# Weight pieces split once and kept in DRAM, and the rotary step of attention moved from GpSimd to VectorE

## The chip, the cores and the metric

The program runs on one core of a Trainium2 chip. The metric is the device time of one execution in microseconds. The kernel before took 1531.3 us (median of three runs, 1529.03 to 1531.97). TensorE is called PE here, its weight loads PEld, VectorE DVE, ScalarE ACT, GpSimd POOL and SyncE SP, as in the profile. PE, DVE, ACT and POOL each work through one queue in order; SP issues most of the DMAs, POOL issues some, among them all that add to their destination.

## The reference

One layer of a streaming encoder, on 2048 prompt tokens and 32 sample tokens, 1024 features, all in float32:

```
h  = RMSNorm(x);  z = h @ W_in          # q k v gA B C u gB mA mB, 5376 columns
q, k = rope(rmsnorm(q)), rope(rmsnorm(k))          # per head of 64; 8 q heads, 2 kv heads
yA = (attend(q, k, v) * silu(gA)) @ W_A # own chunk of 64 tokens and the two before, with sinks
yB = (B * conv3(C * u) * silu(gB)) @ W_B
r  = x + (sigmoid(mA) * yA + sigmoid(mB) * yB) @ W_o
out = r + sigmoid(r @ W_pg) * (p @ W_pp)

rope(x): x1, x2 = halves of the head;  [x1*cos - x2*sin, x2*cos + x1*sin]
rmsnorm(x): x * rsqrt(mean(x*x) + eps) * g
```

The rotary step and the root of the norm belong to one another: the root is one number for each token and head, so it can be multiplied in before the rotation or after it.

## The kernel before, in words

Every float32 product is computed as three matmuls on values split in two: a value v becomes h, v rounded to the format of the matmul, and l = v - h. ACT makes h by a cast and DVE makes l by a subtraction. Weights come from DRAM in pieces of 128 x 512 floats (256 KB, `wr`), four blocks of 128 x 128 each; a piece is split into a tile `w` with both halves. The input `wu` holds the weights in units of eight blocks, so a unit is two pieces. Many products use Strassen-like sums, which take seven products (numbered 1 to 7) for eight; products 1, 2 and 4 use a piece of the weights as it is, products 3, 5, 6 and 7 use sums of pieces, which the kernel forms once and keeps in DRAM (`ws` and `qs`).

The kernel has two parts.

**The steps** (up to about 855 us) compute z = h @ W_in in 21 groups of columns, first for tokens 0 to 1023 (pass 0, products in steps named (0, g, p)) and then for the others (pass 1, steps (1, g, p), with sets of smaller products before and between them). Their results pass through tiles of the pool `tp` (14 tiles named "t", from `tmp`) on their way to DRAM. The order of instructions here is made by the framework's own scheduler from the order in which the program names the work.

**The units** (after that) do attention and the products yB, yA, o (W_o), pg (W_pg) and pp (W_pp), in four blocks of tokens: 0, the two big blocks 1 and 2 together (unit kind "B"), and 3, which ends with quarter-size products (kind "S"). PE goes through the units in the order of the list `plan`. The rest is put into each engine's queue by a planner in the kernel: it keeps a clock of PE (`now`), estimated costs of every operation, and counts of buffers; a task runs when its time is due and its buffers are free, and `next_loads` issues loads ahead of PE. The queues that come out are fixed when the program is built.

**Weights in the units.** `next_loads` loads each piece into one of 8 raw tiles (tag "wf") and `split_w` splits it on ACT and DVE into one of 5 tiles "w". Some pieces are loaded and split several times: those of W_A in blocks 0, 1 with 2, and 3, for instance.

**Attention.** The function `attention` handles 128 tokens (16 such tiles, and one of the 32 sample tokens). PE transposes q, k and v into PSUM (`pq`, `pkv`). ACT squares them into `qn`; DVE sums the squares (`ss`) and adds eps; POOL takes the power -0.5 of `ss` and multiplies the table of cosines and sines `cs` by the gains (`ab`). DVE multiplies q and k by the root into `qn`. POOL multiplies `qn` by `ab` into `tt` (each value times its cosine and times its sine) and adds the halves into `kr` and `qr`. PE transposes `kr` and `qr`, and scores, softmax and the product with V follow.

The attention code that the change replaces on POOL:

```
for h0, hn, q in ((8, 2, 1), (0, 8, 0)):
    eG.tensor_tensor(out=tt[:n, h0:h0 + hn], in0=qn[...], in1=ab[:n, q]..., op=mul)
```

## Time and profile before

| | |
|---|---|
| median of three runs | 1531.3 us |
| the profiled execution | 1532.24 us, its span 1530.5 us |
| PE busy | 1501.7 us (98% of the span) |
| PE weight loads | 1333.8 us (87%) |
| DVE busy | 1206.2 us (79%) |
| ACT busy | 836.3 us (55%) |
| POOL busy | 468.3 us (31%) |
| moved by DMA | 357.94 MB, 234 GB/s over the span |
| granted PE clock | 0.995 |

How to read it: matmuls overlap one another, so a mean duration of one matmul is longer than the time between two of them, and PE's busy time is the union. What PE could still lose or win is its idle time and the time in which the clock is not granted. "Idle before" of a group names what that engine waited for. The table of stretches gives busy time of every engine, the granted clock, the share of time in which the 16 DMA engines were busy (packets of several queues can overlap, so it can exceed 1) and the rate.

### The profile page before, as it was taken

How to read it: one execution, taken by the hardware profiler on the slowest of the kernel's cores; microseconds unless marked ns; L12 is line 12 of the kernel's file. 1: busy time of each engine (PE TensorE's matmuls, PEld its weight loads, DVE VectorE, ACT ScalarE, POOL GpSimd, SP SyncE). 2: the span in 40 equal slices, each digit the busy share in tenths (PEclk: the TensorE clock that was granted, in tenths of full speed). 3: DMA queues.
4: the chain of work that ended last, by engine and by line, in shares of the span. 5: the costliest groups of instructions: out<-in, count | busy, mean ns of one | idle time of the engine just before them, and what ended most of it. 6: DMA issues, size and time to landing. Idle time of an engine off the chain costs nothing.

```text
span 1530.5 us, 27077 instructions
## 1 busy us (share of the span) xinstructions
PE 1501.7 (98%) x9025; PEld 1333.8 (87%) x9025; DVE 1206.2 (79%) x2208; ACT 836.3 (55%) x1966; POOL 468.3 (31%) x634
## 2 busy tenths in 40 slices
PE   9999999999999999999999999989999999999898
PEld 7878888888889999999999889978887877888898
DVE  7896887875589766898955787898967789785886
ACT  8453354344467544434554566767775475653575
POOL 2133332332212232333232245462433334112112
PEclk9999999999999999999999999999999999999999
DMA  9479886798778845343555786685678838879998
GB/s 341 154 280 342 308 293 232 276 342 279 241 266 268 307 141 196 117 132 115 184 191 185 266 302 216 217 245 188 201 193 217 220 93 205 223 209 319 289 311 253
DMA packets 207292, 357.94 MB, mean 234 GB/s; under 512 B 24624, under 2 KB 61552, under 8 KB 207152
## 3 DMA queue, kind: packets, MB, share of 16 engines
q1 hardware_dynamic: 165216, 252.40, 50.9%
q0 software_dynamic: 32288, 85.99, 19.3%
q10 hardware_dynamic: 9648, 17.83, 3.1%
q8 instruction: 71, 1.16, 0.3%
q14 instruction: 69, 0.57, 0.1%
HBM read 238.77 MB, written 117.46 MB: 233 GB/s over the span
## 4 chain that ended last, share of the span: by engine, by line
PE 41%; DVE 5%; DMA 4%; issue 2%; ACT 1%; SPq 0%; POOL 0%; DVEq 0%; ACTq 0%
PE b L135 7%; PE yB L135 6%; PE yA L135 3%; PE o L135 3%; PE pg L135 3%; PE O L135 2%; DMA pf<-in_pT 2%; PE S L135 2%; PE s58a L135 1%; PE la L722 1%; DMA wr<-in_wu 1%; PE a L589 1%; PE a L586 1%; PE a L584 1%; PE s50a L135 1%
## 5 line engine op out<-in xcount | busy, mean ns | idle before, releaser
L586 PE MATMUL a<-x_l,w 128*128 128x264 f32 (+1 forms) x744 | 228.2, 319 | 0.0
L584 PE MATMUL a<-x_h,w 128*128 128x264 f32 (+1 forms) x744 | 227.3, 320 | 0.4 <-DVE s L790 0.4
L589 PE MATMUL a<-x_h,w 128*128 128x264 f32 (+1 forms) x744 | 201.4, 320 | 0.0
L135 ACT CAST w<-wr 128x512 fp32r<-128x512 f32 x204 | 123.7, 621 | 87.2 <-PE b L135 30.9
L135 DVE TENSOR_TENSOR w<-wr,w 128x512 fp32r<-128x512 f32 x204 | 154.0, 765 | 18.3 <-ACT w L135 16.8
L206 ACT CAST w<-wr 128x512 fp32r<-128x512 f32 (+1 forms) x180 | 110.1, 618 | 105.8 <-PE c L589 30.7
L207 DVE TENSOR_TENSOR w<-wr,w 128x512 fp32r<-128x512 f32 (+1 forms) x180 | 131.0, 738 | 36.9 <-ACT w L206 35.6
L584 PEld LDWEIGHTS a<-x_h,w 128*128 128x128 f32 x744 | 139.8, 188 | 11.0 <-DVE s L790 0.6
L586 PEld LDWEIGHTS a<-x_l,w 128*128 128x128 f32 x744 | 140.1, 188 | 10.3
L135 PE MATMUL b<-xb_h,w 128*128 128x512 f32 x448 | 142.7, 395 | 1.8 <-ACT w L135 1.1
L589 PEld LDWEIGHTS a<-x_h,w 128*128 128x128 f32 x744 | 125.2, 188 | 10.8
L722 PE MATMUL la<-x_h,w 128*128 128x264 f32 x516 | 111.9, 285 | 1.7 <-ACT w L206 1.2
L584 PE MATMUL c<-x_h,w 128*128 128x512 f32 (+1 forms) x336 | 110.5, 339 | 0.0
L586 PE MATMUL c<-x_l,w 128*128 128x512 f32 (+1 forms) x336 | 110.4, 338 | 0.0
L135 PEld LDWEIGHTS b<-xb_h,w 128*128 128x128 f32 x448 | 83.4, 188 | 21.0 <-DVE w L135 1.6
L206 ACT CAST w<-a 128x512 fp32r<-128x512 f32 x82 | 49.7, 620 | 94.3 <-DVE a L342 30.9
L589 PE MATMUL c<-x_h,w 128*128 128x512 f32 (+1 forms) x336 | 99.9, 338 | 0.0
L783 DVE SCALAR_TENSOR_TENSOR u<-u,c 128x264 f32<-128x264 f32 (+1 forms) x125 | 59.4, 507 | 42.7 <-ACT u L778 28.4
L778 ACT COPY u<-a 128x264 f32<-128x264 f32 (+1 forms) x114 | 47.4, 437 | 79.7 <-PE a L589 75.5
L135 PE MATMUL yA<-ac_h,w 128*128 128x512 f32 (+1 forms) x320 | 89.0, 358 | 1.6 <-DVE ta L135 1.0
L722 PEld LDWEIGHTS la<-x_h,w 128*128 128x128 f32 x516 | 87.0, 189 | 2.4 <-ACT w L206 1.4
L135 PE MATMUL b<-xb_l,w 128*128 128x512 f32 x224 | 88.3, 394 | 0.0
(535 smaller groups left out, 4310.2 us busy)
## 6 DMA issues: line engine op xcount, KB each, us to landing
wr<-in_wu SPq DMA_DIRECT2D x213, 256.0 KB, 4.2
a<-in_wu SPq DMA_DIRECT2D x116, 256.0 KB, 5.1
wr<-ws SPq DMA_DIRECT2D x74, 256.0 KB, 3.5
wr<-qs SPq DMA_DIRECT2D x64, 256.0 KB, 4.6
ws<-a POOLq DMA_DIRECT2D x63, 256.0 KB, 3.8
qs<-a POOLq DMA_DIRECT2D x24, 256.0 KB, 5.7
tb<-z_t SPq DMA_DIRECT2D x24, 256.0 KB, 4.9
z_t<-tb SPq DMA_DIRECT2D x24, 256.0 KB, 4.3
```

The costliest lines, as they stand in the source:

```text
L135: return f(**kw)
L206: nc.scalar.copy(out=hi, in_=src)
L207: nc.vector.tensor_tensor(out=lo, in0=src, in1=hi.bitcast(F32), op=sub)
L584: nc.tensor.matmul(out=ps[:, :cn], lhsT=w[:, 0, k], rhs=x[0][:, c0:c0 + cn], start=first and k == 0, stop=False, skip_group_check=True)
L586: nc.tensor.matmul(out=ps[:, :cn], lhsT=w[:, 0, k], rhs=x[1][:, c0:c0 + cn], start=False, stop=False, skip_group_check=True)
L589: nc.tensor.matmul(out=ps[:, :cn], lhsT=w[:, 1, k], rhs=x[0][:, c0:c0 + cn], start=False, stop=k == 3, skip_group_check=True)
L722: nc.tensor.matmul(out=ps[:, :m], lhsT=w[:, a, k], rhs=r[:, cols], start=q in "ABG" and j == 0 and e == 0, stop=j == 1 and e == 2, skip_gr ...
L778: nc.scalar.copy(out=t[:, c0:c0 + cn], in_=ps[:, :cn])
L783: nc.vector.scalar_tensor_tensor(out=t[:, c0:c0 + cn], in0=t[:, c0:c0 + cn], scalar=-1.0, in1=ps[:, :cn], op0=mul, op1=sub)
```

## The change

**Stored pieces.** 52 pieces (W_B and W_A of all eight units, W_pp, W_o and W_pg) get a place in DRAM for both halves (`stored`, tiles `wd`, 512 KB each). `store_split` takes three tiles of `tp`, loads a piece on SP, splits it on ACT and DVE, and stores both halves by two DMAs from POOL. The table `store_at` puts these 52 into the steps: 28 into pass 0 from group 9 on, 4 into (1, 5..8, 6), and 20 into groups 16 to 20 of pass 1.

**Units.** Where a piece is stored (`unit_key`), the units load both halves: 512 KB into a "w" tile by one DMA, or into two "wf" tiles by two DMAs, without ACT and DVE. In the built program 128 loads of 256 KB with their splits become 128 loads of 512 KB; the 64 loads of sums `qs` are still split. `room` counts the tiles.

**Plan.** yB and pp of block 2 and 3 alternate; pp of block 3 (n = 2 to 5) moves from the end of the big blocks to between the yA of block 0; yA of block 3 begins earlier among the last products of the big blocks. Two loads of rows of p fall away.

**Attention.** ACT's squares go to a tile `sq` that stands for the whole run and has eps in a 65th column, so that DVE's sum includes it. DVE multiplies q and k out of PSUM by `ab` into `tt`, adds the halves into `kn` and `qr`, and multiplies these by the root at the end (`kr`, `qr`). POOL keeps the power, and `ab`, which is now formed before the squares.

```diff
+    def store_split():
+        u, e = to_store.pop(0)
+        raw = tmp(f"wq{u}_{e}")[:, :512]
+        nc.sync.dma_start(out=raw, in_=wu[u, :, 4 * e:4 * e + 4, :].rearrange("p a b -> p (a b)"))
+        h, lo = [tmp(f"wq{x}{u}_{e}", F32R)[:, :512] for x in "hl"]
+        split(h, lo, raw)
+        for i, v in enumerate((h, lo)):
+            nc.gpsimd.dma_start(out=stored[u, e][:, i], in_=v.bitcast(F32).rearrange("p (a b) -> p a b", a=4))
...
+    store_at = {(0, g, p): 1 for g in range(9, G) for p in (6, 3) if p == 6 or g > 11}
+    store_at.update({(0, g, 5): 1 for g in range(14, G)})
+    store_at.update({(1, g, p): 1 for g in range(5, 9) for p in (6,)})
+    store_at.update({(1, g, p): 1 for g in range(16, G) for p in (1, 6, 7, 5)})
...
-        while n_raw[0] < len(worder) and busy["Y"] < now[0] + 0.5 and (
-                n_raw[0] < RAWS or raw_free[n_raw[0] - RAWS] <= now[0]) and n_raw[0] < len(made) + RAWS:
-            i = n_raw[0]
+        while n_load[0] < min(len(worder), used[0] + LOOK) and busy["Y"] < now[0] + 0.5:
+            i = n_load[0]
+            key = worder[i]
...
+            if unit_key(key):
+                where = "w" if room["w"] > len(to_split) else "wf"
+                if where == "wf" and room["wf"] < 3:
+                    break
+                src = stored[unit_key(key)]
+                tiles = w_tiles(i, where)
+                if where == "w":
+                    eY.dma_start(out=whole[i].bitcast(F32), in_=src)
+                else:
+                    for v in range(2):
+                        eY.dma_start(out=tiles[v].bitcast(F32), in_=src[:, v])
+                w_ready[i] = fin[0] + 0.5
...
-    plan += tail[:21]
-    for e, part in enumerate(tail[21:]):
-        plan += [part, ("yA", 3, NA[3][e])]
-    plan += [("pp", 3, 2), ("pp", 3, 3), ("yA", 3, NA[3][7]), ("pp", 3, 4), ("pp", 3, 5)]
+    plan += tail[:17]
+    late = [("yA", 3, n) for n in NA[3]]
+    for e, part in enumerate(tail[17:27]):
+        plan += [part] + ([late.pop(0)] if e not in (2, 9) else [])
+    plan.append(tail[27])
...
         for h0, hn, src in q3:
-            eS.activation(out=qn[:n, h0:h0 + hn], in_=src[:n], func=AF.Square, scale=SCALE)
+            eS.activation(out=sq[:n, h0:h0 + hn, 0:64], in_=src[:n], func=AF.Square, scale=SCALE)
...
+        for q, (h0, hn, src) in enumerate(q3):
+            eV.tensor_tensor(out=tt[:n, h0:h0 + hn], in0=src[:n].unsqueeze(2).to_broadcast([n, hn, 2, 64]),
+                            in1=ab[:n, q].unsqueeze(1).to_broadcast([n, hn, 2, 64]), op=mul)
...
-        eV.tensor_reduce(out=ss[:n], in_=qn[:n], axis=AX.X, op=add)
-        eV.tensor_scalar(out=ss[:n], in0=ss[:n], scalar1=EPS, scalar2=None, op0=add)
+        eV.tensor_reduce(out=ss[:n], in_=sq[:n], axis=AX.X, op=add)
...
+        for d in (0, 32):
+            for o, h in ((kn, slice(8, 10)), (qr, slice(0, 8))):
+                eV.tensor_tensor(out=o[:n, :, d:d + 32], in0=tt[:n, h, 0, d:d + 32], in1=tt[:n, h, 1, 32 - d:64 - d], op=add)
...
-        for h0, hn, src in q3[::-1]:
-            eV.tensor_tensor(out=qn[:n, h0:h0 + hn], in0=src[:n], op=mul,
-                            in1=ss[:n, h0:h0 + hn].unsqueeze(2).to_broadcast([n, hn, 64]))
...
-        for h0, hn, q in ((8, 2, 1), (0, 8, 0)):
-            eG.tensor_tensor(out=tt[:n, h0:h0 + hn],
-                            in0=qn[:n, h0:h0 + hn].unsqueeze(2).to_broadcast([n, hn, 2, 64]),
-                            in1=ab[:n, q].unsqueeze(1).to_broadcast([n, hn, 2, 64]), op=mul)
...
+        eV.tensor_tensor(out=kr[:n], in0=kn[:n].unsqueeze(2).to_broadcast([n, 2, 2, 64]),
+                        in1=ss[:n, 8:10].unsqueeze(2).unsqueeze(3).to_broadcast([n, 2, 2, 64]), op=mul)
+        eV.tensor_tensor(out=qr[:n], in0=qr[:n], in1=ss[:n, 0:8].unsqueeze(2).to_broadcast([n, 8, 64]), op=mul)
```

**How the queues move.** Three places. The first is the rotary step of the first tile of block 2 (names with `2_0`), on POOL, before:

```order
L135 TENSOR_TENSOR ss2_0_12274<-ss2_0_12274,nhalf_70 128x10
L135 TENSOR_TENSOR ab2_0_12316<-cs2_0_12091,cst_69 128x256
L135 DMA ta0_4_12121<-z_t1_4_112 128x512
L135 TENSOR_TENSOR tt2_0_12383<-qn2_0_12261,ab2_0_12316 128x256
L135 DMA ta0_5_12166<-z_t1_5_113 128x512
L135 TENSOR_TENSOR tt2_0_12383<-qn2_0_12261,ab2_0_12316 128x1024
L135 TENSOR_TENSOR kr2_0_12385<-tt2_0_12383 128x4x32 x2
L135 TENSOR_TENSOR qr2_0_12384<-tt2_0_12383 128x8x32 x2
L135 COPY KH_10068<-KH_10068 128x2x128
L135 COPY KL_10069<-KL_10069 128x2x128
```

and on POOL now:

```order
L135 TENSOR_TENSOR ab2_0_12757<-cs2_0_12656,cst_69 128x256
L135 DMA ta0_3_12574<-z_t1_3_111 128x512
L135 TENSOR_TENSOR ss2_0_12796<-ss2_0_12796,nhalf_70 128x10
L135 DMA ta0_4_12649<-z_t1_4_112 128x512
L135 COPY KH_10522<-KH_10522 128x2x128
L135 COPY KL_10523<-KL_10523 128x2x128
```

The products and sums of the rotation are gone from POOL; the power `ss` and `ab` have stayed. On DVE the same tile now has these rows (`m0` are values of block 0 being split, `pf` rows of p, `ta` the yA of block 0, `VL` the low half of v, `at` and `ptl` attention of earlier chunks):

```order
L135 TENSOR_TENSOR tt2_0_12763<-pq2_0_12749,ab2_0_12757 128x1024
L135 TENSOR_TENSOR tt2_0_12763<-pkv2_0_12754,ab2_0_12757 128x256
L135 TENSOR_REDUCE ss2_0_12796<-sq_10534 128x10
L135 SCALAR_TENSOR_TENSOR m0_1_l_12773<-ta0_1_12430,m0_1_h_12772 128x512
...
L135 TENSOR_TENSOR kn2_0_12765<-tt2_0_12763 128x2x32
L135 TENSOR_TENSOR qr2_0_12764<-tt2_0_12763 128x8x32
L135 TENSOR_TENSOR kn2_0_12765<-tt2_0_12763 128x2x32
L135 TENSOR_TENSOR qr2_0_12764<-tt2_0_12763 128x8x32
L135 TENSOR_TENSOR ptl_13_0_12874<-PT_13_0_12868,pth_13_0_12873 128x512
L135 TENSOR_TENSOR kr2_0_12766<-kn2_0_12765,ss2_0_12796 128x256
L135 TENSOR_TENSOR qr2_0_12764<-qr2_0_12764,ss2_0_12796 128x512
```

where it had two products before, `qn` out of PSUM by the root, between which and POOL's rows nothing else of the tile stood on DVE:

```order
L135 SCALAR_TENSOR_TENSOR m0_2_l_12326<-ta0_2_12014,m0_2_h_12325 128x512
L135 TENSOR_TENSOR qn2_0_12261<-pkv2_0_12253,ss2_0_12274 128x128
L135 TENSOR_TENSOR qn2_0_12261<-pq2_0_12248,ss2_0_12274 128x512
L135 SCALAR_TENSOR_TENSOR ta0_5_12166<-ta0_5_12166,yA0_5_0_12285 128x512
L135 TENSOR_TENSOR KL_10069<-pk1_3_12328,KH_10068 128x2x128
```

So DVE has nine rows of the rotation instead of two, the first two of which read PSUM and wait for no root.

The second place is SP late in pass 0, at the loads of group 19 (`a19`), before:

```order
L330 DMA wr130_3775<-in_wu 128x512
L330 DMA a19_0_3832<-in_wu 128x512
L330 DMA a19_1_3834<-in_wu 128x512
L330 DMA a19_2_3836<-in_wu 128x512
L330 DMA a19_3_3838<-in_wu 128x512
L330 DMA wr136_3904<-in_wu 128x512
```

and now, with `wq` the pieces to be stored (their stores, two each, stand on POOL):

```order
L334 DMA wr130_3963<-in_wu 128x512
L334 DMA a19_0_4044<-in_wu 128x512
L334 DMA a19_1_4046<-in_wu 128x512
L374 DMA wq49_0_3825<-in_wu 128x512
L334 DMA a19_2_4048<-in_wu 128x512
L334 DMA a19_3_4050<-in_wu 128x512
L374 DMA wq66_0_3851<-in_wu 128x512
```

Loads of pieces to be stored stand between the loads that the group itself needs. The third place is SP at the change from W_o to W_pg in block 3 (units "S"; `z_r` and `r` are rows of r), before:

```order
L135 DMA wr520_17514<-in_wu 128x512
L135 DMA wr521_17535<-in_wu 128x512
L135 DMA z_r1_93<-r013_0_17069 128x544
L135 DMA wr522_17559<-in_wu 128x512
L135 DMA wr523_17567<-in_wu 128x512
L135 DMA z_r5_97<-r113_1_17207 128x544
L135 DMA wr524_17591<-in_wu 128x512
```

and now:

```order
L135 DMA w520_17765<-wd67_1_164 128x1024
L135 DMA w521_17787<-wd58_0_173 128x1024
L135 DMA wh522_17790<-wd58_1_189 128x512
L135 DMA wl522_17791<-wd58_1_189 128x512
L135 DMA w523_17811<-wd59_0_174 128x1024
L135 DMA w524_17831<-wd59_1_190 128x1024
```

Each of these pieces is now 128 x 1024 floats, in one load or in two.

More of the change, by code (lines that the diff above doesn't have):

```diff
@@ L1191, in tile_hybrid_stream_step @@
             quad_sums(*sums_at[todo[0]])
+        for _ in range(store_at.get(todo[0], 0)):
+            store_split()
         if i in after:
@@ L1218, in tile_hybrid_stream_step @@
         nc.gpsimd.memset(v.bitcast(F32), 0.0)
+    sq = att.tile([P, 10, 65], F32, tag="sq", name="sq")
+    nc.gpsimd.memset(sq, EPS)
     restart()
@@ L1779, in run_big @@
         for k in range(4):
-            while ("XB", x, p, k) not in have or wi >= len(w_ready) or w_ready[wi] > now[0]:
+            while ("XB", x, p, k) not in have or w_ready.get(wi, 1e9) > now[0]:
                 idle()
-            hi, lo = made[wi][:, 0, k], made[wi][:, 1, k]
+            hi, lo = [v[:, k] for v in W2[wi]]
             xh, xl = XB[x, p, k]
@@ L1793, in run_big @@
                 free("kx", 2)
-        over.add(widx.pop(wk))
-        while n_done[0] in over:
-            n_done[0] += 1
+        w_over(wk)
         go(big_done(u, ps), now[0] + SEM, BIG_NEED.get((x, p)), -1)
@@ L2076, in run_quads @@
                 i, half = XP[p]
-                while ("X", x, i, k) not in have or wi >= len(w_ready) or w_ready[wi] > now[0]:
+                while ("X", x, i, k) not in have or w_ready.get(wi, 1e9) > now[0]:
                     idle()
@@ L2089, in run_quads @@
                 if k == 3:
-                    over.add(widx.pop(wk))
-                    while n_done[0] in over:
-                        n_done[0] += 1
+                    w_over(wk)
         for n, p in u["parts"]:
@@ L2160, in tile_hybrid_stream_step @@
     widx = {}
-    n_raw, n_hi, n_made, n_done = [raws[0]], [len(made)], [len(made)], [used[0]]
-    landed = {i: 3.0 for i in range(raws[0])}
-    raw_free = [6.0 if i < len(made) else 1e9 for i in range(raws[0])]
-    w_ready = [0.5] * len(made)
-    base = used[0]
+    W2 = {i: (made[i][:, 0], made[i][:, 1]) for i in range(used[0], len(made))}
+    w_ready = {i: 0.5 for i in W2}
+    room = {"w": WB - len(W2), "wf": 8}
+    slot = {i: "w" for i in W2}
+    n_load, to_split, landed, whole = [len(made)], [], {}, {}
     def w_of(key, u):
@@ L2231, in tile_hybrid_stream_step @@
+            n_load[0] += 1
+        if to_split and landed[to_split[0]] <= now[0] and room["w"] > 0 and now[0] >= hold[0] and busy["S"] < now[0] + (
+                0.3 if to_split[0] > used[0] + 2 else 1.5):
+            go(split_w(to_split.pop(0)))
     work = [0.0]
     last_use = {k: x for x, u in enumerate(units) for k in u["w"]}
-    over = set()
     def run_units():
@@ L2257, in run_units @@
                     wi = w_of(wk, u)
-                    while key not in have or wi >= len(w_ready) or w_ready[wi] > now[0]:
+                    while key not in have or w_ready.get(wi, 1e9) > now[0]:
                         idle()
                     k = i % 4 + (2 * (u["n"] % 2) if wk[0] == "pp" else 0)
-                    hi, lo = made[wi][:, 0, k], made[wi][:, 1, k]
+                    hi, lo = [v[:, k] for v in W2[wi]]
                     a = operand(key)
```

127 lines of the change are left out of this document (74 added, 53 removed).

## The prediction, made before the changed kernel was run

> **What bounds the kernel now.** I read the busy times first, then the stretches of the span in which PE is idle, then what PE waits for, and last what DVE and POOL do at those moments. The page's first line:
>
> ```profile
> PE 1501.7 (98%) x9025; PEld 1333.8 (87%) x9025; DVE 1206.2 (79%) x2208; ACT 836.3 (55%) x1966; POOL 468.3 (31%) x634
> ```
>
> PE is the bound, and the change leaves its matmuls alone. All that can be won is idle PE time, 1530.5 - 1501.7 = 28.8 us, plus lower-clock time. The stretches show where it lies (length, busy time of PE, PEld, DVE, ACT and POOL, then the granted clock, the share of busy DMA engines and the rate):
>
> ```profile
> 325.00:350.00 25.00, 25.00 (x110) 20.28 (x109) 17.86 (x30) 10.92 (x20) 7.04 (x13) 1.00 0.98 354
> 337.00:465.00 128.00, 128.00 (x634) 107.57 (x632) 86.48 (x160) 64.02 (x120) 25.92 (x49) 1.00 0.79 266
> 465.00:525.00 60.00, 57.76 (x463) 56.50 (x462) 50.75 (x104) 42.41 (x96) 18.39 (x28) 1.00 0.88 304
> 750.00:850.00 100.00, 99.42 (x816) 99.21 (x815) 63.93 (x133) 54.79 (x117) 21.46 (x24) 1.00 0.63 205
> 1000.00:1034.00 34.00, 28.21 (x158) 23.96 (x157) 33.43 (x48) 20.79 (x59) 21.40 (x22) 1.00 0.84 223
> 1155.00:1175.00 20.00, 17.13 (x82) 13.37 (x82) 16.92 (x26) 14.24 (x44) 11.22 (x11) 0.91 0.90 264
> 1240.00:1265.00 25.00, 21.77 (x107) 17.51 (x106) 22.38 (x35) 17.00 (x47) 13.99 (x16) 1.00 0.37 96
> 1400.00:1436.00 36.00, 30.59 (x204) 27.62 (x203) 29.69 (x59) 17.72 (x36) 7.84 (x9) 1.00 1.08 317
> 1433.00:1525.00 92.00, 89.19 (x688) 87.90 (x688) 76.63 (x152) 59.53 (x126) 15.67 (x18) 0.98 0.95 288
> ```
>
> In the steps (to 855 us) PE hardly idles. Three stretches of attention lose 5.8, 2.9 and 3.2 us, 11.9 in all; 1400 to 1436 us loses 5.4. PE's two longest waits (total, times, longest), then DVE and then POOL around them (start, duration):
>
> ```profile
> PE S L135 <- DVE qs L135: 5.5, 2, 3.8
> PE yA L135 <- DVE ac_l L135: 2.9, 1, 2.9
> ```
> ```profile
> 1006.37 3.79 DVE L135 TENSOR_TENSOR w<-wr,w 128x512 fp32r<-128x512 f32 x2
> ...
> 1023.50 0.68 DVE L135 SCALAR_TENSOR_TENSOR m_l<-ta,m_h 128x512 fp32r<-128x512 f32 x1
> 1027.24 4.92 DVE L135 SCALAR_TENSOR_TENSOR m_l<-ta,m_h 128x512 fp32r<-128x512 f32 x1
> 1165.33 4.74 DVE L135 SCALAR_TENSOR_TENSOR ac_l<-acf,ac_h 128x512 fp32r<-128x512 f32 x2
> ```
> ```profile
> 1026.09 0.89 POOL L135 DMA_DIRECT2D ta<-z_t  x1 [0.82 <-DVE KL L135]
> 1026.69 2.70 POOL L135 TENSOR_TENSOR tt<-qn,ab 128x1024 f32<-128x1024 f32 x1
> 1029.06 1.15 POOL L135 TENSOR_TENSOR kr<-tt 128x128 f32<-128x128 f32 x2
> 1029.89 1.65 POOL L135 TENSOR_TENSOR qr<-tt 128x256 f32<-128x256 f32 x2
> 1165.55 3.35 POOL L135 TENSOR_TENSOR tt<-qn,ab 128x256 f32<-128x256 f32 x2
> ```
>
> The same DVE instruction takes 0.68 us alone and 4.92 us while POOL runs `tt`, `kr`, `qr`; it ends (1032.16) as they do (1031.54). DVE is 98% busy in that stretch, so `qs`, queued behind it, comes late, and PE with it. The second wait has the same form. So the unit losses from 1000 to 1265 us come from POOL's rotary step holding up DVE.
>
> From 1400 us it is something else. The chain of waits there runs through DMAs (start, length):
>
> ```profile
> 1373.44 10.34 DMA wr<-in_wu
> ...
> 1392.56 7.58 DMA ta<-z_t
> 1400.15 11.15 DMA pf<-in_pT
> ...
> 1413.38 7.94 DMA pf<-in_pT
> ```
>
> against a usual landing of 4.2 us (the page: `wr<-in_wu SPq DMA_DIRECT2D x213, 256.0 KB, 4.2`), in a stretch whose DMA share is 1.08.
>
> **The change part by part.** Three groups of rows carry the counts (instructions, busy time, mean ns; from 855 us on):
>
> ```profile
> L135 ACT CAST w<-wr 128x512 fp32r<-128x512 f32 x188 | 114.0, 621 | 79.5 <-PE b L135 30.9 <-PE yA L135 16.2 <-PE yB L135 11.3
> L135 DVE TENSOR_TENSOR w<-wr,w 128x512 fp32r<-128x512 f32 x188 | 143.4, 771 | 16.8 <-ACT w L135 15.4 <-DMA wr<-in_wu 0.5
> L135 DVE TENSOR_TENSOR qn<-pq,ss 128x512 f32<-128x512 f32 x16 | 10.9, 680 | 0.0
> L135 DVE TENSOR_TENSOR KL<-pk,KH 128x256 fp32r<-128x256 f32 x16 | 6.7, 416 | 1.0 <-ACT KH L135 1.0
> L135 DVE TENSOR_TENSOR qn<-pkv,ss 128x128 f32<-128x128 f32 x16 | 4.5, 284 | 0.1
> L135 DVE TENSOR_TENSOR VL<-pkv,VH 64x64 fp32r<-64x64 f32 x64 | 14.1, 220 | 2.8 <-ACT vo L135 1.3 <-ACT VH L135 0.7
> L135 POOL TENSOR_TENSOR tt<-qn,ab 128x1024 f32<-128x1024 f32 x16 | 41.8, 2613 | 0.0
> L135 POOL TENSOR_TENSOR ss<-ss,nhalf 128x10 f32<-128x10 f32 x16 | 32.7, 2044 | 114.8 <-DVE ss L135 100.0 <-DVE se L135 14.7
> L135 POOL TENSOR_TENSOR qr<-tt 128x256 f32<-128x256 f32 x32 | 27.1, 929 | 0.0
> L135 POOL TENSOR_TENSOR kr<-tt 128x128 f32<-128x128 f32 x32 | 21.4, 771 | 0.0
> ```
>
> *A: the rotary step, with the splits of the units.* POOL loses 2.6 us of `tt`, 1.9 of `qr` and 1.5 of `kr` a tile, beside the small `tt`. DVE gains two products out of PSUM, four sums and two multiplications. The product of 1024 does not stand in the trace: from the rows of 512 and 256 elements the slope is (0.680 - 0.416)/256, so 0.680 + 512 slopes = 1.21 us (twice 0.680 at most). The rest: `tt` of 256, 0.42; sums, 2 x 0.22 and 2 x 0.42; `kr`, 0.42; `qr`, 0.68. Together 4.0 us, less the two `qn` rows and the addition of eps (some 1.1): +2.9 a tile, about 49 us over 17 tiles. Against it stand 128 splits: 128 x 0.771 = 98.7 us of DVE and 128 x 0.621 = 79.5 of ACT. DVE is lighter by about 50 us in the units, and its long blocks lose their partner. What that can bring is the idle time of the three stretches, 11.9, and the time lost at the lower clock behind the stall at 1166, 20 x (1 - 0.91) = 1.8: 13.7 us. It can bring nothing if DVE is late for another reason. I take 10: POOL keeps the power `ss` (2.0 us a tile) and `ab`, so some blocks remain, and the new rows come in one burst a tile.
>
> The Trainium skill (page "SBUF — State Buffer", section "Who interferes with whom") gives the reason: a DVE operation with two SBUF inputs and a GpSimd operation share one pair of ports under an exclusive lock, and the second waits. The 4.92 against 0.68 us agree. By it the new sums and the splits can still be held by `ss` and `ab`.
>
> *B: from 1350 to 1436 us.* 16 of the stored pieces fall there (16 x 0.26 = +4.2 MB), while pp 2 to 5 of block 3, with rows of p and results (about 2.7 MB), leave it:
>
> ```profile
> 1350.00:1433.00 83.00, 79.37 (x452) 69.31 (x451) 62.34 (x111) 41.24 (x77) 19.19 (x22) 1.00 1.02 291
> ```
>
> 24.2 MB become 25.7, or 309 GB/s, still under the 354 of the best stretch. The `pf` loads of the chain are those that move, and splits leave DVE. Between 0 and the 5.4 us of idle time I take -3: late loads are only partly cured by fewer of them.
>
> *C: the steps.* Each stored piece is 0.26 MB read and 0.52 written, 0.786 in all, with a split on ACT and DVE and three tiles of `tp`. DVE (86.48 of 128 us) and ACT (64.02) have room for 21 splits, and POOL (25.92) for 42 stores of 0.89 us each, the time of one issue above; but a store waits for its split, and POOL's other stores, which free tiles of `tp` and feed later groups, stand behind it. The DMA is closer: 21 pieces fall from 337 to 465 us, so 34.0 + 16.5 = 50.5 MB, which at 354 GB/s take 142.7 us, 14.7 too many. From 750 to 850 us 20 pieces make 20.5 + 15.7 = 36.2 MB, 102.3 us, 2.3 too many. Bounds: 0, if stores and loads simply drift later, and 17, if PE waits for all of it. The drift has room: 465 to 525 us could move 3.0 MB more, 8.5 us of the excess, and in the row at 354 GB/s PE is busy for 25.00 of 25.00 us. That row is the nearest, so I take +2.
>
> The Trainium skill (page "DMA: Bandwidth & Descriptors", section "Specifications") has about 358 GB/s as the limit of HBM for a core; the 354 lie just under it. By its figure the excess in pass 0 is an estimated 13 us, all of it a loss if nothing drifts; it speaks against the change.
>
> *D: the end, 1433 to 1525 us.* 24 stored pieces and one more load add 6.6 MB to 26.5: 33.1 MB, 93.4 us at 354 GB/s and 104 at the 317 of the stretch in which PE waited for loads. A loss of 0 to 12 us; I take +4, because the present losses here (2.8 us of 92) are small and 93.4 is the nearer of the two times to what the row needs. Fewer splits help but DVE, with 76.63 of 92, was not what ran out.
>
> **Sum.** 1532.24 (the profiled execution: its span 1530.5 and 1.7 around it) - 10 - 3 + 2 + 4 = 1525.2. The median of the three runs lies 0.9 lower, so 1524. The main case without the ends reaches from 1515 to 1530.
>
> **The rivals.**
>
> *R1, slower: the DMA engines become the bound.* Stores of both halves in the steps and loads twice as large in the last 175 us meet a DMA that is already 0.79 to 1.08 busy. PE waits for loads behind the stores in pass 0 (+17) and in the quarter products (+12); A holds, B is lost: 1532.24 - 10 + 17 + 12 - 0.9 = 1550, own range 1537 to 1557. It decides from the point at which the loads of a group can no longer be issued ahead of PE, since `wq` loads and the group's share SP's queue and the pool `tp`. For it: 50.5 MB do not fit into 128 us. Against it: the row at 354 GB/s without idle PE.
>
> *R2: nearly all idle time of the units goes.* A -13.7, B -5.4, C and D 0: 1532.24 - 19.1 - 0.9 = 1512. For it: DVE is 50 us lighter just where it was the queue in front of PE. Against it: `ss`, `ab` and the long landings stay.
>
> *R3: no change, as DVE's own bursts take the place of the blocks.* Four us of rotation a tile stand in DVE's queue in one piece, ahead of `qs`, `m_l` and `ac_l`, about as long as the blocks (4.92, 4.74). A is only -3: 1532.24 - 3 - 3 + 2 + 4 - 0.9 = 1531. Against it: the burst does not lie at the same places, and 128 splits less let DVE catch up.
>
> That the change does not do what it says is excluded by the orders of the queues: the rows of the rotation are gone from POOL and stand on DVE.
>
> **How the numbers follow.** Main case 0.46, R1 0.20, R2 0.20, R3 0.14. About 0.2%, 3 us, is what a measurement tells from no change here. Faster: the main case, nearly all of it, R2, and little of R3, 0.66; the same: most of R3 and the upper edge of the main case, 0.11; slower: R1 and a few of R3, 0.23. The range for 8 in 10 goes from 1508 (R2's sum and the 3 us by which the runs differ) to 1546 (into R1, half of its own range).
>
> **What would show it.** *A is right* if POOL's rows `tt`, `kr`, `qr` are gone, no DVE row with two SBUF inputs takes 4 us any more, and PE idles less than 5 us in the attention that now takes 11.9. *B* if the chain from 1350 us has no `pf` or `wr` of 7 us or more. *C* if the steps end as before, about 855 us, with 337 to 465 us near 354 GB/s and PE still whole; R1 if PE names DMAs there, with idle time of 10 us. *D* if loads of 512 KB in the last 92 us land near the 4.2 us of the smaller ones plus 0.7, the time for another 256 KB at 354 GB/s; if they take 10, PE's waits name `w<-wd`. The prediction is wrong altogether if the steps lose more than 10 us, or if the last 92 us grow by more than 8.

## The result: 1582.5 us, 3.3% slower

| | before | changed |
|---|---|---|
| median | 1531.6 us (4 runs) | 1582.5 us (4 runs, 1578.5 to 1584.0) |
| ratio, 95% interval | | 1.033 (1.0305 to 1.0355) |
| profiled execution, its span | 1532.2, 1530.5 us | 1581.1, 1579.3 us |
| moved by DMA | 357.9 MB, 234 GB/s | 431.9 MB, 273 GB/s |
| granted PE clock | 0.995 | 0.984 |

The forecast was 1524 us and the range ended at 1546. The page of the changed kernel:

```profile
PE 1515.6 (96%) x9025; PEld 1341.5 (85%) x9025; DVE 1163.9 (74%) x2215; ACT 794.2 (50%) x1888; POOL 423.8 (27%) x637
```

DVE, ACT and POOL are all lighter, as they were meant to be, and PE idles for 63.7 us in place of 28.8. The other 14 of the 49 us are busy time: the same matmuls take 1515.6 us in place of 1501.7, at a granted clock of 0.984 in place of 0.995. To see where, both traces are cut at the same numbers of matmuls: 2400 (late in pass 0), 5600 (the first units) and 8000 (ahead of the quarter products). Before, and then changed (length, busy time of PE, PEld, DVE, ACT, POOL, clock, DMA share, GB/s):

```profile
0.00:508.00 508.00, 503.50 (x2398) 417.93 (x2399) 400.55 (x691) 254.98 (x495) 136.24 (x254) 1.00 0.81 280
508.00:923.00 415.00, 413.99 (x3204) 403.38 (x3204) 315.59 (x631) 201.58 (x470) 131.39 (x174) 1.00 0.59 190
923.00:1377.00 454.00, 442.12 (x2405) 376.88 (x2404) 374.58 (x664) 296.26 (x831) 171.84 (x175) 0.99 0.72 202
1377.00:1530.00 153.00, 142.08 (x1024) 135.58 (x1022) 115.52 (x226) 83.50 (x171) 28.78 (x33) 0.99 0.98 294
```
```profile
0.00:539.00 539.00, 512.71 (x2397) 421.49 (x2398) 417.70 (x719) 270.19 (x523) 168.02 (x311) 0.98 0.87 306
539.00:971.00 432.00, 419.87 (x3202) 407.24 (x3201) 332.73 (x659) 205.31 (x474) 140.33 (x206) 0.99 0.70 235
971.00:1403.00 432.00, 431.82 (x2408) 371.60 (x2406) 316.58 (x646) 256.26 (x763) 82.63 (x85) 1.00 0.84 255
1403.00:1579.00 176.00, 151.20 (x1025) 141.18 (x1023) 96.85 (x195) 62.40 (x128) 32.81 (x38) 0.95 1.01 315
```

The first two stretches are the same work in both kernels: +31 and +17 us. In the third and fourth the plan has exchanged products, so their lengths are to be compared as a sum (607.5 and 608.3 us) and each alone by PE's idle time: from 11.9 to 0.2 in the third, from 10.9 to 24.8 in the fourth. (The expectations below give these as 30 and 17 us lost, 23 won and 22 lost, counted at equal numbers of matmuls.) So the attention has become as whole as it can be, and the steps and the end have lost far more. PE's waits now (total, times, longest):

```profile
PE a L616 <- ACT u L810: 6.8, 4, 3.2
PE a L616 <- ACT s L810: 5.7, 2, 5.5
PE s50b L135 <- DMA w<-wd: 4.4, 1, 4.4
```

`u` and `s` are ACT's copies of a finished product out of PSUM. What stands ahead of one in ACT's queue:

```profile
444.44 0.62 ACT L206 CAST wqh<-wq 128x512 fp32r<-128x512 f32 x1 [3.23 <-DMA wq<-in_wu]
444.97 0.58 ACT L810 COPY s<-a 128x512 f32<-128x512 f32 x1
```

Here a cast of a piece waits for the piece's load, the copy stands behind it, and PE waits 5.5 us for the copy. Whether such waits make up the loss is tried below. At the end of the steps the chain of waits goes from piece to piece:

```profile
837.51 5.39 DMA wq<-in_wu
...
849.87 6.17 DMA wq<-in_wu
861.54 7.78 DMA wq<-in_wu
873.54 6.36 DMA wd<-wqh
...
887.60 5.51 DMA wq<-in_wu
```

### The profile page after: what moved, and what is told of

Its sections match the earlier page's. It is cut to its first block, busy times and chain, and to the rows that moved or that the text cites. A ratio compares the mean times of both kernels' runs of the same rounds, so it can differ in the third digit from the quotient of the medians.

```text
span 1579.3 us, 27248 instructions
## 1 busy us (share of the span) xinstructions
PE 1515.6 (96%) x9025; PEld 1341.5 (85%) x9025; DVE 1163.9 (74%) x2215; ACT 794.2 (50%) x1888; POOL 423.8 (27%) x637
## 4 chain that ended last, share of the span: by engine, by line
PE 41%; DMA 11%; issue 3%; DVE 2%; ACT 1%; POOL 0%; SPq 0%; DVEq 0%; POOLq 0%; ACTq 0%
PE b L135 8%; PE yB L135 5%; PE yA L135 4%; PE o L135 3%; PE pg L135 3%; DMA wr<-qs 2%; PE O L135 2%; DMA wq<-in_wu 2%; PE la L754 2%; PE S L135 2%; PE a L621 2%; PE a L616 2%; PE a L618 2%; DMA pp<-z_pp 2%; PE PT L135 1%
## 5 line engine op out<-in xcount | busy, mean ns | idle before, releaser
L616 PE MATMUL a<-x_h,w 128*128 128x264 f32 (+1 forms) x744 | 231.3, 324 | 15.7 <-ACT u L810 6.8
L621 PE MATMUL a<-x_h,w 128*128 128x264 f32 (+1 forms) x744 | 202.5, 322 | 0.7 <-DVE w L207 0.7
L207 DVE TENSOR_TENSOR w<-wr,w 128x512 fp32r<-128x512 f32 (+1 forms) x176 | 134.2, 772 | 29.8 <-ACT w L206 28.7
L135 PE MATMUL b<-xb_h,w 128*128 128x512 f32 x360 | 115.1, 395 | 0.0
L135 PEld LDWEIGHTS b<-xb_h,w 128*128 128x128 f32 x360 | 67.2, 188 | 14.8
L135 ACT CAST w<-wr 128x512 fp32r<-128x512 f32 x80 | 48.9, 620 | 56.2 <-DMA wr<-qs 29.7
L815 DVE SCALAR_TENSOR_TENSOR u<-u,c 128x264 f32<-128x264 f32 (+1 forms) x125 | 59.3, 506 | 23.4 <-PE c L621 11.9
L754 PE MATMUL la<-x_l,w 128*128 128x264 f32 x258 | 74.4, 289 | 0.9 <-DVE x_l L207 0.9
L207 DVE TENSOR_TENSOR w<-a,w 128x512 fp32r<-128x512 f32 x82 | 55.2, 686 | 22.4 <-ACT w L206 22.2
L135 PE MATMUL b<-xb_l,w 128*128 128x512 f32 x180 | 70.9, 394 | 0.0
```

Source lines behind the costliest of these rows:

```text
L135: return f(**kw)
L207: nc.vector.tensor_tensor(out=lo, in0=src, in1=hi.bitcast(F32), op=sub)
L616: nc.tensor.matmul(out=ps[:, :cn], lhsT=w[:, 0, k], rhs=x[0][:, c0:c0 + cn], start=first and k == 0, stop=False, skip_group_check=True)
L621: nc.tensor.matmul(out=ps[:, :cn], lhsT=w[:, 1, k], rhs=x[0][:, c0:c0 + cn], start=False, stop=k == 3, skip_group_check=True)
L754: nc.tensor.matmul(out=ps[:, :m], lhsT=w[:, a, k], rhs=r[:, cols], start=q in "ABG" and j == 0 and e == 0, stop=j == 1 and e == 2, skip_gr ...
L815: nc.vector.scalar_tensor_tensor(out=t[:, c0:c0 + cn], in0=t[:, c0:c0 + cn], scalar=-1.0, in1=ps[:, :cn], op0=mul, op1=sub)
```

## Experiments

The change has three parts that can be built apart: the rotary step, the stored pieces, and the new plan. Below, "first stretch" and so on are the four above. Ratios are to the kernel before. A kernel for which no interval is given was timed once; the four runs of the changed kernel lie within 5.5 us, so differences of that size between such kernels tell nothing.

**The rotary step alone.** The attention part of the diff on the kernel before, nothing else:

```diff
+eV.tensor_tensor(out=tt..., in0=src (PSUM), in1=ab...)   # and the sums, and the root at the end
-eG.tensor_tensor(out=tt..., in0=qn..., in1=ab...)
```

> The kernel before with the attention part of the change alone: the rotary step on DVE out of PSUM, no stored pieces, the old plan of units and the old loads and splits. In the changed kernel the stretch from 1000 to 1400 us won 23 us. Theory A (POOL's rotary step held DVE up, and that alone): this kernel wins it by itself, 1531 - 15 to 24 = 1507 to 1516 us, and PE's idle time from 1000 to 1265 us falls from 11.9 to under 3 us. Rival (DVE and ACT are lighter by 128 splits, and that is what emptied their queues): with the splits still there the win is small, 1525 to 1531 us, or none, since DVE now has 49 us more to do.

Measured: 1534.7 us, ratio 1.0030 (1.0019 to 1.0041), so a little slower. Its third stretch:

```profile
921.00:1377.00 456.00, 444.93 (x2404) 378.74 (x2404) 372.01 (x737) 304.91 (x857) 88.59 (x90) 0.99 0.73 200
```

POOL's busy time there falls from 171.8 to 88.6 us and PE's idle time only from 11.9 to 11.1. The expectation's theory A, that POOL's rotary step alone held DVE up, falls: the blocks are gone and the time isn't. PE now waits for `ptl`, `ac_l` and `m_l` (7.6 us) on a DVE that has its own rotation in its queue, and 3.2 us for ACT. DVE's busy time in this stretch is 372.0 us and was 374.6: its new rows, which take 50 us more than those that they replace, come close to the time for which POOL had held it up.

**What costs 48 us in the steps.** Two theories: the DMA engines are full, or casts that wait in ACT's queue hold up PE's results. First without casts and without their two tiles, then with casts and without the stores:

```diff
-        split(h, lo, raw)
-        for i, v in enumerate((h, lo)):
-            nc.gpsimd.dma_start(out=stored[u, e][:, i], in_=v...)
+        for i in range(2):
+            nc.gpsimd.dma_start(out=stored[u, e][:, i], in_=raw...)
```

> The changed kernel, but the steps store the 52 pieces as they were loaded, twice, without cast and subtraction (so both halves in DRAM hold the whole value, and the products of the units with stored pieces are not the reference's; loads, stores and their bytes are the same). The steps with the first units lost 47 us (30 by 510 us, 17 from 827 to 935 us). Theory ACT (the cast of a piece waits in ACT's queue for the piece's load, and the copies that free PSUM for PE stand behind it): the loss of the steps falls under 10 us, about 1540 us. Theory DMA (52 pieces of 0.79 MB do not fit through the DMA engines in these stretches): the loss stays at 35 us or more, about 1575 to 1582 us.

```diff
         split(h, lo, raw)
-        for i, v in enumerate((h, lo)):
-            nc.gpsimd.dma_start(out=stored[u, e][:, i], in_=v...)
```

> The changed kernel, but the 52 pieces are loaded and split in the steps and not written, and the units load and split every piece as before (so the steps have their casts and 0.26 MB a piece in place of 0.79). Without casts the changed kernel lost 15 us by 510 us and 3 from 827 to 907 us, with them 30 and 17. Theory ACT: the casts still wait for their loads, and 12 us or more of the 30 stay. Theory DMA: the bytes written fill the engines, and without them under 5 us stay. The attention with all splits and the rotary step on DVE should lose what it lost with the rotary step alone: PE idle for 12 us or more from the first units to 1270 us.

Measured: 1553.2 us without casts, 1545.3 us without stores (and with all splits in the units). First and second stretch of the one without casts, then of the one without stores:

```profile
0.00:524.00 524.00, 507.21 (x2397) 418.64 (x2398) 399.48 (x692) 254.34 (x496) 168.56 (x311) 0.99 0.88 315
524.00:942.00 418.00, 414.61 (x3208) 403.98 (x3206) 317.01 (x635) 193.66 (x451) 140.66 (x205) 1.00 0.72 243
```
```profile
0.00:524.00 524.00, 507.12 (x2398) 417.14 (x2399) 416.12 (x720) 269.82 (x523) 136.86 (x255) 0.99 0.82 287
524.00:948.00 424.00, 417.10 (x3207) 406.01 (x3206) 335.80 (x667) 210.99 (x478) 113.15 (x156) 1.00 0.63 202
```

In the first stretch each leaves 16 of the 31 us, so each theory has about a half there; that the halves add is arithmetic, as no run went without both, and the run without casts has fewer tiles as well. In the second stretch the bytes alone cost 3 us and the casts with a third of the bytes 9, of 17 together.

Which property of the casts is it? Two guesses were tried, each on the whole change: the load three to six steps earlier, so that a cast finds its piece landed, and two tiles a piece in place of three.

```diff
+        store_load()                            # the DMA of the piece
+        late_at[i + (3 if i < 141 else 6)] = 1  # cast, subtraction and stores so many steps later
```

> The changed kernel, but a piece is loaded three steps (8 us) before its split in pass 0 and six steps (8 us) before it in pass 1; the bytes and the casts are the same, and its first tile is held 8 us longer. Theory ACT: the casts find their pieces landed; the loss of the steps falls from 47 us to what it was without casts, 19 us, and the whole to 1552 to 1558 us. Theory DMA: no change, 1576 us or above. Theory tiles (the three tiles of a piece, of 14, are missing elsewhere): worse, 1585 us or above.

```diff
-        h, lo = [tmp(f"wq{x}{u}_{e}", F32R)[:, :512] for x in "hl"]
+        h, lo = tmp(f"wqh{u}_{e}", F32R)[:, :512], raw.bitcast(F32R)
```

> The changed kernel, but the low half of a stored piece is written over the piece itself, so a piece holds two of the 14 tiles in place of three; loads, casts, stores and steps are the same. Theory tiles (what the next steps need waits for tiles): the 28 to 31 us lost by 540 us fall to 22 or less. Theory bytes and casts: 26 or more stay.

Measured: 1582.1 us with early loads and 1579.0 us with two tiles. First stretch with early loads, then with two tiles (the second stretches are 431 and 429 us long):

```profile
0.00:539.00 539.00, 513.27 (x2404) 422.89 (x2405) 416.60 (x720) 269.16 (x524) 167.81 (x311) 0.98 0.87 306
```
```profile
0.00:541.00 541.00, 510.85 (x2401) 420.60 (x2402) 418.19 (x721) 269.67 (x523) 167.40 (x311) 0.98 0.87 305
```

Neither is it: both are as the changed kernel. Early loads did to the casts what they were meant to. What the work on the pieces waited for their loads, in the changed kernel and with early loads (us, times, over the whole program):

```profile
  DMA wq<-in_wu: 50.4, 27
```
```profile
  DMA wq<-in_wu: 7.6, 4
```

That wait is nearly gone and the time is the same, so the waits of casts for their own loads, as at 444 us above, do not by themselves make up the loss (unless the piece's first tile, held 8 us longer here, costs just as much).

Half of the 31 us are lost in one place. Its two ends are 1800 and 2000 matmuls, before and then changed:

```profile
421.00:457.00 36.00, 36.00 (x206) 31.52 (x205) 29.28 (x61) 22.89 (x46) 5.37 (x10) 1.00 0.79 274
```
```profile
433.00:485.00 52.00, 40.83 (x200) 33.77 (x198) 34.87 (x69) 28.14 (x55) 13.43 (x25) 0.90 0.95 331
```

PE comes to this place 12 us late, lost bit by bit from about 305 us on, and loses 16 more in it, 5 of them as busy time at the lower clock. It comes late by 8 and loses 7 without casts, 5 and 9 without stores, 14 and 13 with early loads, 10 and 20 with two tiles. What stands there are loads of the other half's values: `xr` uses tiles of the same pool and stands in SP's queue with the pieces. The first of them, before and with two tiles a piece (rows of SP's queue, start and length):

```profile
424.75 1.02 SPq L575 DMA_DIRECT2D xr<-xc  x2
```
```profile
449.75 0.93 SPq L614 DMA_DIRECT2D xr<-xc  x2
```

With two tiles ACT then waits for them, and PE 13.3 us for ACT's `x_h`:

```profile
456.29 1.16 ACT L206 CAST x_h<-xr 128x528 fp32r<-128x528 f32 x2 [11.92 <-DMA xr<-xc]
```

In the changed kernel PE waits only 2.4 us for `x_h` there, after the 5.5 us for the copy. The first `xr` is issued 21 us later than before in the changed kernel (445.8), 16 without casts (440.8), 9 without stores (433.9), 24 with early loads and 25 with two tiles; PE itself is 12, 8, 5, 14 and 10 us late just ahead, so a part of that is only the lateness of all. The place of half the loss is shown; why these loads fall back further, and what loses the rest, is not settled: the rotation of the shared tiles, SP's order and late values on DVE are not told apart.

**Other places for the pieces.** One kernel spreads the 52 over pass 1, two give them five tiles of their own:

```diff
-    store_at = {(0, g, p): 1 for g in range(9, G) for p in (6, 3) if p == 6 or g > 11}
+    store_at = {i: 1 for i in [*range(165, 249, 3), *range(262, 342, 10), *range(345, 409, 4)]}
```

> The changed kernel with its 52 pieces stored at other steps: 28 of them evenly in what was 520 to 630 us before, 8 up to 745 us, 16 up to 830 us, where DMA moved 85 to 280 GB/s and PE was whole; none in pass 0 and none in the last steps. Theory DMA: loads land in their usual time there and the loss of the steps falls from 47 us to under 8, 1535 to 1543 us. Theory ACT: each cast still waits for its own load, 4 us or so, and PE loses a part of that at most pieces, 20 us or more in all, 1555 us or above. In both the last 150 us stay as they are in the changed kernel, 22 us longer than before.

```diff
-        raw = tmp(f"wq{u}_{e}")[:, :512]
+        raw = qp.tile([P, 512], F32, tag="q", name=f"wq{u}_{e}")   # a pool of 5; h, lo as well
```

> The changed kernel, but the three tiles of a stored piece come from a pool of five of their own and no longer from the 14 that the results and the loads of the other half's values share; bytes, casts and steps are the same. With bytes and casts the steps lost 27 to 31 us by 540 us, without casts 16, without the stores 16, and loading earlier changed nothing. Theory tiles (a piece holds three of 14 tiles until its stores land, and what the next steps need is loaded and copied later for it): the 30 fall to 16 or less. Theory DMA with ACT (each bears half: full engines, and casts in ACT's queue): 26 or more stay. A pool of five can itself make a piece wait, which would add to the loss.

> As the run without casts (pieces stored twice as they were loaded, so the products of the units with stored pieces are not the reference's), but their tile is one of five of their own: what is left of the edit in the steps are its loads and stores alone. Theory DMA: the 16 us of the run without casts were its bytes, and 13 or more of them stay by 540 us. Theory tiles: they were its tile, and under 8 us stay.

Measured: 1596.3 us spread over pass 1 (ratio 1.0432, 1.0399 to 1.0466), 1589.5 us with tiles of their own, 1587.3 us with tiles of their own and without casts. Neither did what was meant. The loads of the pieces in pass 1, and in the last of the three (number, ns, first and last start):

```profile
L374 SPq DMA_DIRECT2D wq<-in_wu x52: 327/383/1995, 459.2 to 854.2; - x52
```
```profile
L374 SPq DMA_DIRECT2D wq<-in_wu x52: 327/328/1407, 27.5 to 263.7; - x52
```

The first starts at 459 us, where 304 GB/s flowed before (465 to 525 us), and not at 520. With tiles of their own the pieces move to the beginning: the first load is issued at 27 us with casts and without, the last at 444 us with casts and at 264 without. So the shared pool is a part of what ties a piece to its step, and these two kernels tell nothing of what the tiles cost. The last one comes nearest to a price of bytes, though SP's order and POOL's issues go with them. Its row from 50 to 275 us, and that of the kernel before:

```profile
50.00:275.00 225.00, 195.42 (x793) 153.68 (x792) 153.57 (x248) 79.01 (x153) 105.05 (x197) 0.92 1.02 385
```
```profile
50.00:275.00 225.00, 224.91 (x976) 181.56 (x975) 185.23 (x303) 100.25 (x198) 65.61 (x121) 1.00 0.79 273
```

There are no casts in it, the DMA share is 1.02, and PE idles for 29.6 us: the pieces were not hidden where 273 GB/s flowed already.

**The end.** The quarter products load 256 KB and split, all else as changed:

```diff
     def keep(key):
-        return True
+        return key[0] != "S"    # stored pieces are not used by the quarter products
```

> The changed kernel, but the quarter products of block 3 load their 24 pieces as before, 256 KB each, and split them on ACT and DVE; all else, the stores and the big blocks with them, stays. The last 150 us lost 22 us. Theory DMA in the tail (loads twice as large in a full DMA): the loss falls under 6 us, 1558 to 1566 us. Rival (the new plan: rows of z and r, pp and the late yA come later and the quarter products begin without them, whatever their weights): it stays, 1575 us or above, with PE idle between 1450 and 1475 us as it is now.

Measured: 1565.6 us. The fourth stretch, which was 176.3 us with 24.8 idle:

```profile
1400.00:1564.00 164.00, 148.31 (x1026) 139.05 (x1024) 111.79 (x219) 75.25 (x152) 33.03 (x38) 0.97 1.00 301
```

So 12 us are the doubled loads of 24 pieces. In the changed kernel they land late, and those that they stand among a little later than before (KB each, median us from issue to landing; fourth stretch of the changed kernel, then of the one before):

```profile
w<-wd SPq DMA_DIRECT2D x17, 512.0 KB, 9.1
wr<-qs SPq DMA_DIRECT2D x32, 256.0 KB, 6.4
```
```profile
wr<-qs SPq DMA_DIRECT2D x32, 256.0 KB, 5.6
wr<-in_wu SPq DMA_DIRECT2D x31, 256.0 KB, 6.1
```

**The attention.** With the rotary step back on POOL, stored pieces and plan as changed:

```diff
-        for q, (h0, hn, src) in enumerate(q3):
-            eV.tensor_tensor(out=tt..., in0=src..., in1=ab...)
+            eG.tensor_tensor(out=tt..., in0=qn..., in1=ab...)
```

> The changed kernel with the rotary step as before, on POOL after the root; stored pieces, plan and all else as changed. From 1000 to 1400 us the changed kernel won 23 us, and the rotary step on DVE alone won nothing. Theory A2 (each needs the other: only a DVE without the splits can take the rotary step, and only then POOL's blocks go): the blocks come back, the win falls under 10 us, 1592 us or above. Rival (the splits alone did it: a lighter DVE bears the blocks): the win stays at 16 us or more, 1575 to 1588 us.

Measured: 1584.9 us; the third stretch has 4.3 us idle in 439:

```profile
967.00:1406.00 439.00, 434.69 (x2403) 373.18 (x2402) 295.90 (x566) 253.38 (x755) 159.12 (x163) 1.00 0.84 251
```

So two thirds of the idle time go without the rotary step on DVE. The run without stores, which has all splits, the rotary step on DVE and the new plan, has 3.9 idle in 439 us as well, where its expectation was 12 or more:

```profile
948.00:1387.00 439.00, 435.09 (x2400) 371.61 (x2399) 363.08 (x723) 296.77 (x849) 88.26 (x85) 0.99 0.74 206
```

What these two share is the plan. It was taken alone, with the rotary step, and with eight pieces:

```diff
     stored = {(u, e): dram.tile([P, 2, 4, P], F32, ...)
-              for us, es in ((range(UY, UY + 8), (1, 0)), ...)
+              for us, es in ()
```

> The changed kernel without stored pieces: the new plan of units, the rotary step on DVE, and all pieces loaded with 256 KB and split in the units. If plan and rotary step together have most of the win, and the steps and the end lose nothing, PE is idle for about 4 us in the attention in place of 11.9, and the kernel takes 1518 to 1524 us, below both kernels and at or below the run with 20 pieces (1525.6). If the stored pieces have the win, 1527 to 1533 us.

> The kernel before with the new plan of units alone (with its loads ordered as in the changed kernel): rotary step on POOL, no stored pieces. Theory P (the plan has the win: it spreads the work of the units): 1518 to 1525 us, as the run beside it. Theory PR (the rotary step on DVE pays only where the plan leaves DVE room, and without it POOL's blocks of 3 to 5 us stay): 1527 to 1534 us, with DVE instructions of over 3 us in the attention.

```diff
+              for us, es in ((range(UY, UY + 8), (0,)),)
```

> As the run with plan and rotary step, with the eight pieces of W_A stored at eight of the last hundred steps, two tiles each. They save 24 of 128 splits. If the idle time left in the attention comes from DVE and ACT being full there, 2 to 4 us of it go and the steps lose 1 to 2: within 3 us of the run beside it on either side. If pieces cost more than they bring at any number, it is 3 to 6 us slower than that run.

| kernel | median us | ratio, 95% interval |
|---|---|---|
| new plan, rotary step on POOL | 1521.6 | 0.9945 (0.9928 to 0.9961) |
| new plan, rotary step on DVE | 1522.6 | 0.9953 (0.9937 to 0.9969) |
| new plan, rotary step on DVE, 8 pieces of W_A | 1534.7 | 1.0030 (1.0017 to 1.0042) |

The plan has the win, 9.5 us. ("The plan" includes here the changed rule by which units load their pieces ahead; the two were not parted. Nor were stored pieces tried with the old plan.) Third and fourth stretch of the plan alone, and two rows of DVE in it:

```profile
922.00:1361.00 439.00, 433.67 (x2399) 371.92 (x2399) 357.01 (x647) 292.82 (x829) 173.93 (x170) 1.00 0.73 207
1361.00:1520.00 159.00, 147.91 (x1028) 139.96 (x1026) 122.10 (x237) 84.61 (x170) 33.09 (x38) 0.97 0.98 281
```
```profile
1200.22 4.27 DVE L135 TENSOR_TENSOR w<-wr,w 128x512 fp32r<-128x512 f32 x2
...
1236.56 2.85 DVE L135 SCALAR_TENSOR_TENSOR xb_l<-tk,xb_h 128x512 fp32r<-128x512 f32 x1
```

POOL is as busy as before (173.9 us), and instructions of 0.68 us still take up to 3.7 (the first row is two of them; before, the longest took 4.9). PE's idle time is 5.3 in place of 11.9 us, and its waits for DVE come to 2.7 in place of 12.0: with the products in this order PE waits less behind a held-up DVE. Whether that is more the order or the somewhat shorter blocks is not told apart. About 4 us more of the win are busy time of PE, 1497.8 in place of 1501.7 us for the same matmuls. With the rotary step moved as well PE idles for 3.4 us, and the time is the same:

```profile
923.00:1362.00 439.00, 435.65 (x2403) 372.12 (x2402) 363.42 (x723) 297.67 (x850) 88.25 (x86) 0.99 0.73 206
```

The run with eight pieces is 12 us slower than the one without, more than its expectation allowed and slower than with 20 pieces below. It loses 5 us up to the first units, 4 in the attention and 4 at the end; why eight cost more than 20 is open.

**Fewer pieces.** 20 pieces (W_B, W_A, W_pp), at steps with room, in four forms: loaded early, with tiles of their own, at later steps with two tiles, and as the last with rows loaded three units ahead. A fifth has 12 pieces with tiles of their own.

```diff
-    for us, es in ((range(UY, UY + 8), (1, 0)), (range(UPP, UPP + 2), (0, 1)), (range(UO, UPG + 8), (0, 1)))
+    for us, es in ((range(UY, UY + 8), (1, 0)), (range(UPP, UPP + 2), (0, 1)))
-    LEAD, AHEAD_S, LOOK = 2, 5, 11
+    LEAD, AHEAD_S, LOOK = 3, 5, 11     # the fourth form only
```

> The changed kernel with 20 stored pieces in place of 52, those of W_B, W_A and W_pp, which are used twice or three times; spread over steps from what was 550 to 825 us before, each loaded six steps before its split; the pieces of W_o and W_pg are loaded and split as before, those of the quarter products too. 48 of the 128 splits are saved. By both theories the steps lose under 4 us. If the attention needs a lighter DVE and gets it with 48 splits fewer, 10 to 18 us are won there and the tail loses 5: 1518 to 1528 us, below both kernels. Rival (48 are too few, DVE stays full from 975 to 1050 us): 1531 us or above.

> The kernel with 20 stored pieces (1528 us, where the steps and the first units lost 9.5 us and the attention won 23), with a pool of five tiles of their own for the pieces. Theory tiles: the loss of the steps falls under 5 us, 1520 to 1525 us. Theory DMA with ACT: it stays, 1526 to 1531 us.

> As the kernel with 20 stored pieces and tiles of their own, with 12 pieces: those of W_A and W_pp; W_B is loaded and split as before. 32 of 128 splits are saved. If the attention wins as much with 32 as with 48, 1517 to 1524 us, since eight pieces less are stored; if DVE is full again from 975 to 1050 us, as it was with the rotary step alone, 5 to 10 us of the win are lost, 1525 to 1532 us.

> The kernel with 20 stored pieces (W_B, W_A, W_pp; 1528 us), each split right after its load and with two tiles, at later steps: 8 pieces in what was 560 to 650 us before, 12 from 720 to 850 us. In that kernel the steps and the first units lost 9.5 us (4 before 550 us, 3 at 650 to 775, 4 at the first units). If pieces cost nothing where DMA has room and PE's loads are not behind them, the steps lose under 4 us in all and the kernel takes 1520 to 1525 us; if each piece costs its own wait anywhere, it stays at 1526 to 1531 us.

> As the run with 20 pieces at later steps, with the rows of a unit loaded up to three units ahead of PE in place of two. From 1400 us the kernel with 20 pieces lost 8 us against before, with DVE waiting 5.8 us for rows of z that took 9.7 us to land. If those rows are merely issued late, 4 to 8 us of it are won against the run beside it; if DMA is full there, earlier loads only push others back: no change within 2 us, or a loss.

| kernel | median us | ratio, 95% interval |
|---|---|---|
| 20 pieces, loaded early | 1528.2 | 0.9987 (0.9974 to 0.9999) |
| 20 pieces, tiles of their own | 1542.1 | 1.0075 (1.0060 to 1.0090) |
| 12 pieces, tiles of their own | 1535.4 | 1.0030 (1.0020 to 1.0041) |
| 20 pieces, later steps, two tiles | 1525.6 | 0.9970 (0.9959 to 0.9981) |
| the same, rows three units ahead | 1525.5 | 0.9965 (0.9954 to 0.9976) |

Tiles of their own sent the pieces to the beginning again. At later steps 20 pieces leave the first stretch as it was, and the other three read:

```profile
509.00:929.00 420.00, 414.98 (x3197) 404.25 (x3196) 325.76 (x654) 202.62 (x470) 134.92 (x198) 1.00 0.70 234
929.00:1361.00 432.00, 431.80 (x2409) 371.75 (x2408) 346.72 (x694) 282.68 (x812) 84.76 (x85) 1.00 0.78 226
1361.00:1524.00 163.00, 147.08 (x1024) 139.26 (x1022) 116.43 (x226) 79.11 (x159) 32.84 (x38) 0.97 0.98 287
```

Against plan and rotary step without pieces (414, 439 and 158 us) the attention wins 7, the steps with the first units lose 6 and the end 5. So 20 pieces in these places bring nothing: 3 us more than plan and rotary step, a difference within the intervals. Rows loaded further ahead change nothing. The lowest medians are those of the plan by itself and with the rotary step: 1522 us, below the kernel before and the changed one.

## Why the prediction was wrong

The sum by the runs: plan -9.5 us (1521.6 against 1531.2 beside it), rotary step +1 (within the intervals), 52 pieces about +60 (1582.5 - 1522.6). The 60 are 30 in pass 0 (539 against 509 us), 18 up to the first units (432 against 414) and 11 after them, where the end loses 18 and the attention wins 7.

- **C failed most: "+2", bounds 0 to 17, measured 48.** Two steps of it failed. The first is that the excess of bytes would drift into a calmer stretch: the run without casts, with the same bytes, lost 16 us in pass 0. That 14.7 us too many had been worked out for it is close by luck. The figure rests on 354 GB/s as the most that the DMA moves, and this run moved 373 GB/s from 337 to 465 us, at which the 50.5 MB need 135 us, 7 too many:

```profile
337.00:465.00 128.00, 122.47 (x535) 99.36 (x534) 77.28 (x137) 55.02 (x99) 47.84 (x89) 0.97 1.01 373
```

  The second is that splits, stores and tiles were priced at nothing, because DVE, ACT and POOL had room on average: with the casts and without the stores pass 0 lost 16 us as well. How the casts cost that stays open; with most of their waits for loads taken away the time was the same. From 750 us the bytes were priced at 2.3, and cost 3; the rest of the 17 came with the casts.
- **A had the size of the win and not its cause, which is luck: "-10" for the rotary step off POOL with fewer splits; moved alone the step cost 5 us (ratio 1.0030), and with the new plan 1.** The blocks were read rightly, and they did go. That their time would be won was the error: DVE was late anyway, since 50 us of new rows (49 had been estimated) took the place of the time for which it had been held. This was the third rival, to which 0.14 was given. The fewer splits bring, under the new plan, PE's idle time from 3.4 to 0.2 us; with the old plan splits and rotary step were not tried together.
- **The new plan was priced only where it moved transfers (B).** For the attention, where it brings what A was to bring, no term of the sum stood. The order of PE's work was quoted in the change and then read for its DMAs alone.
- **B: "-3" from 1350 to 1436 us, none of it seen.** With the plan alone PE idles for 11.1 us in the last stretch, 10.9 before. The loads of `pf` have left the chain of waits there, but `pp<-z_pp` of 11.9 us and `wr<-qs` of 9.6 stand in it now.
- **D: "+4", bounds 0 to 12, measured 12 for the quarter products' loads alone** (176 against 164 us), the upper bound that 317 GB/s gave: the rate of the stretch was 315. The row in which PE already waited for loads was the nearer one, and the stretch as a whole did not reach 354 GB/s. Another 5 or 6 us go with the other stored pieces (164 here, 163 with 20 pieces, 158 without any).
- **The first rival was nearest, and too small.** Its sign came true, and its two places: pass 0 (17 said, 30 measured) and the quarter products (12 said, 12 measured). It had nothing for the end of the steps, where 17 us were lost, and held A for won. Its condition, that loads of a group can no longer be issued ahead of PE because `wq` loads share SP's queue and the pool, fits the late `xr`; it is not shown.
- **Signs that were named ahead**: POOL's rows are gone and PE idles for 0.2 us in the attention, as A asked for. The steps end 48 us later, and the last stretch has lost over 8, the two signs of being wrong altogether. 300 to 450 us runs at 343 to 355 GB/s, but PE is not whole there. PE's waits name the DMA less than they name ACT, which the forecast did not look for.

## What to carry to other kernels

Work put into a stretch where the bound engine is whole is not priced by busy shares: here DVE, ACT and POOL had room and 48 us were lost. Ask what stands behind it in each queue that it joins, and whose loads share its tiles; which of these cost most here was not settled. When a stall ends with a slowed instruction, see whether the engine would be late without the slowing; if it is full, moving work onto it changes the name of the wait and not the time. A change of several parts should be priced part by part with the order of the bound engine's own work among them: here that one was the only net gain.
